# Two FFN products by seven quarter products each, with the second one's activations passed through device memory

## The chip, the cores and the metric

One core of a Trainium2 chip runs the kernel. TensorE (PE) multiplies, VectorE (DVE), ScalarE (ACT) and GpSimd (POOL) do the elementwise work, SyncE (SP) and the other queues issue DMAs. The metric is the device time of one execution: the kernel before took 2033.25 us (median of 3 runs, 2033.06 to 2033.38). All arithmetic is fp32; a product is made from high and low parts of both operands, as three matmuls (high by high, high by low, low by high).

## The reference, cut to what matters

One decoder layer over 1056 rows (a prompt of 1024 and 8 samples of 4), model width 1024. The change touches the last third of it; what goes before (conv, S5 and attention branches, their merge) is left as it is.

```python
x = x + g_m * rmsnorm(merged @ p['w_out'], p['g_post_mix'])
hf = rmsnorm(x, p['g_pre_ffn']) * (1.0 + sc_f) + sh_f
gu = hf @ p['w_ffn_in']                       # 1024 -> 2 * 2816
f = jax.nn.silu(gu[..., :D_FF]) * gu[..., D_FF:]
x = x + g_f * rmsnorm(f @ p['w_ffn_out'], p['g_post_ffn'])   # 2816 -> 1024
```

Outputs are the new x, and states and K/V rows that the earlier stages write.

## The kernel before, in words

Activations lie transposed (features on the 128 partitions, rows along the free axis). A tile of weights is 128 x 128 per matmul; the moving operand is a chunk of 352 rows (three chunks, `csl`), or of 264 rows (four chunks, `lsl`) in the last part.

The program is a list of `Atom`s that `run` (L369) goes through: an atom is one group of matmuls into one PSUM bank. Its evacuation is held back as `pending` and written out after the next atom's matmuls. A `unit` is 512 KB of weights: SP loads it into `raw`, ACT writes the high part `whi` (L396), DVE the low part `wlo` (L397); `ready` allows a unit when a buffer of its ring of three is free. Work beside the matmuls stands in generators that `Side` holds: `advance` steps them by the estimated cost of each atom, and `drain` runs them to their end at that place of the program. Each engine works its own list in the order in which the program wrote it, so what stands first on an engine and waits holds all that is behind it.

- w_out (from `plain(open_r)`): 3 chunks of 8 atoms of 24 matmuls; weights 3 to 7 are kept over the chunks. `sq_gated` squares and gates a bank, `res_gen` (L1826) makes for each finished chunk the two norms, the residual and the modulated input of the FFN, split into `mh` (high) and `ml` (low). Its norms go by way of PE twice: a sum over the partitions (`s<-cst,ss`, `s<-cst,y`), 13 small DVE operations and a diagonal (`rs_dg`), and a matmul that spreads the result (`s<-rs_dg`).
- FFN in and out, in five parts of `PARTS = (4, 4, 5, 4, 5)` tiles of features: for each tile the gate and the up product (24 matmuls of 352 rows for each chunk), tanh, two products on DVE, the split into `fhi` and `flo`; after a part its share of the second product is added into `ya`.
- the last part goes in four chunks of 264 rows, each followed by `last_gen`: norm, residual and output.

In the FFN of the kernel before POOL issues a few DMAs, and shares the last residuals.

Of the kernel before, what the change touches and what calls it, by code (L numbers as in the profile page):

```python
# [16 lines left out]
T = 1056  # L17
# [28 lines left out]
YF = (1.0, 4.0, 0.64)  # L46

# [70 lines left out]
def layout(inp):  # L118
# [3 lines left out]
    o['xT'] = x.reshape(3, CH, 8, 128).transpose(0, 3, 2, 1)  # L122
    c = np.concatenate([g['c_prompt'], g['c_sample']], 0)
# [135 lines left out]
def program(tc, I, O):  # L259
# [39 lines left out]
    xd = dram.tile([128, 8, T], F32, name="xd")  # L299
    numd = [dram.tile([128, 2, TP], F32, name="numd%d" % g) for g in range(2)]  # L300
# [3 lines left out]
    def mm(out, lhsT, rhs, start, stop):  # L304
        return pe.matmul(out=out, lhsT=lhsT, rhs=rhs, start=start, stop=stop)  # L305
# [37 lines left out]

    def kept(box, pool_):

        def get(ask=False):
            if ask:
                return box.get(pool_)
            n_kept[0] += 1
            hi = box[pool_].tile([128, 1024], F32R, name="kh%d" % n_kept[0])  # L350
            if pool_ == 'kp':
                return hi, lo_tile(F32R, "kl")[:, 0:1024]
# [1505 lines left out]
    for c in range(NCH):  # L1858
        for m in range(8):
            u = us[m]  # L1860

            def evac(ps, c, m=m):
# [3 lines left out]
                if m == 7:  # L1866
                    if c:
                        side.drain()
# [162 lines left out]
```

## Time and profile before

| | us |
|---|---|
| median of 3 runs | 2033.25 |
| the profiled execution | 2028.49 |
| its span | 2026.7 |
| from w_out's first matmul to the end (1118.0 to 2026.7) | 908.7 |
| PE busy, share of the span | 96% |
| DVE, ACT, POOL busy | 53%, 29%, 8% |

A stage is read from the views of busy time in stretches; PE counts as busy from a matmul's start to its modelled end, and consecutive matmuls overlap, so the pace of a stage is time divided by count. The idle time in front of an instruction is shown in brackets with what ended it.

### The profile page before, as it was taken

Reading aid. Unit: us, or ns where it says so; the run is one execution under the profiler, and the core shown is the slowest. Engines: PE = TensorE matmul, PEld = TensorE weight load, DVE = VectorE, ACT = ScalarE, POOL = GpSimd, SP = SyncE. Lnnn points to the kernel's source line nnn. Section 1 sums busy time; section 2 is a strip of 40 time slices with the busy share of each in tenths; the row PEclk is TensorE's granted clock in tenths of the full one; section 3 lists DMA queues with packets and bytes.
Section 4 is the critical chain, followed back from the end, with each engine's and each line's share of the span. In section 5 each row is a group of like instructions: output and inputs, shape, how many; then the busy total and the mean of one; then the engine's idle time right before and its main releaser. Section 6 shows DMA issues by size and latency. Waiting matters only on the chain.

```text
span 2026.7 us, 29823 instructions
## 1 busy us (share of the span) xinstructions
PE 1951.0 (96%) x12284; PEld 1824.4 (90%) x12284; DVE 1078.7 (53%) x2256; ACT 586.6 (29%) x1145; POOL 159.6 (8%) x273
## 2 busy tenths in 40 slices
PE   8999999999999899999999998999999999999997
PEld 2899798798876788998999998999999999999996
DVE  5677685474474766654976378312332233232347
ACT  3422422522422542222323344232202111212233
POOL 0000001001000131223200000000000000000023
PEclk9999999999999999999999999999999999999998
DMA  7333134134355544226732222110111011111131
GB/s 286 88 105 108 45 126 147 55 116 154 116 189 195 189 147 138 93 93 188 195 101 80 91 107 79 52 53 32 52 53 42 27 58 53 42 53 41 52 108 76
DMA packets 59847, 203.88 MB, mean 101 GB/s; under 512 B 12372, under 2 KB 13540, under 8 KB 58176
## 3 DMA queue, kind: packets, MB, share of 16 engines
q1 hardware_dynamic: 35264, 110.70, 16.3%
q0 software_dynamic: 17104, 64.82, 9.4%
q10 hardware_dynamic: 7344, 26.47, 3.9%
q8 instruction: 96, 1.57, 0.3%
q14 instruction: 39, 0.32, 0.0%
HBM read 159.87 MB, written 43.00 MB: 100 GB/s over the span
## 4 chain that ended last, share of the span: by engine, by line
PE 56%; DVE 3%; issue 2%; DMA 2%; ACT 1%; POOL 1%; POOLq 0%; DVEq 0%; ACTq 0%
PE z L305 53%; PE s L305 3%; DMA yq<-yd 1%; DVE y L308 1%; POOL Tm L1338 0%; DMA yd<-ysb 0%; DMA raw<-i_wfo 0%; DMA sbw<-i_sb 0%; ACT mh L615 0%; DMA raw<-i_wout 0%; DVE x L1824 0%; DVE wlo L397 0%; DVE ss L308 0%; PE m L305 0%; DVE kl L397 0%
## 5 line engine op out<-in xcount | busy, mean ns | idle before, releaser
L305 PE MATMUL z<-hh,whi 128*128 128x352 f32 x1152 | 380.5, 330 | 2.7 <-ACT hh L615 1.4
L397 DVE SCALAR_TENSOR_TENSOR wlo<-raw,whi 128x1024 fp32r<-128x1024 f32 (+1 forms) x169 | 203.3, 1205 | 329.1 <-ACT whi L396 324.9
L305 PE MATMUL z<-hh,wlo 128*128 128x352 f32 x1152 | 373.1, 324 | 3.1 <-DVE wlo L397 3.1
L305 PE MATMUL z<-hl,whi 128*128 128x352 f32 x1152 | 373.2, 324 | 0.8 <-DVE hl L308 0.8
L305 PE MATMUL z<-mh,whi 128*128 128x352 f32 x1104 | 358.9, 325 | 4.6 <-ACT mh L615 4.6
L305 PE MATMUL z<-ml,whi 128*128 128x352 f32 x1104 | 358.2, 324 | 0.3 <-DVE ml L308 0.2
L305 PE MATMUL z<-mh,wlo 128*128 128x352 f32 x1104 | 357.9, 324 | 0.0
L396 ACT ACTIVATE whi<-raw 128x1024 fp32r<-128x1024 f32 (+1 forms) x169 | 176.0, 1042 | 396.9 <-PE z L305 341.7
L305 PEld LDWEIGHTS z<-hh,whi 128*128 128x128 f32 x1152 | 219.3, 190 | 14.5 <-issue 7.0
L305 PEld LDWEIGHTS z<-hh,wlo 128*128 128x128 f32 x1152 | 219.1, 190 | 3.7 <-DVE wlo L397 3.7
L305 PEld LDWEIGHTS z<-hl,whi 128*128 128x128 f32 x1152 | 219.3, 190 | 2.6 <-DVE hl L308 1.6
L305 PEld LDWEIGHTS z<-mh,whi 128*128 128x128 f32 x1104 | 208.8, 189 | 5.5 <-ACT mh L615 5.1
L305 PEld LDWEIGHTS z<-ml,whi 128*128 128x128 f32 x1104 | 209.0, 189 | 1.7 <-DVE ml L308 1.4
L305 PEld LDWEIGHTS z<-mh,wlo 128*128 128x128 f32 x1104 | 208.8, 189 | 0.0
L305 PE MATMUL z<-fhi,whi 128*128 128x352 f32 (+1 forms) x504 | 161.0, 319 | 2.9 <-DVE ya L308 2.9
L305 PE MATMUL z<-fhi,wlo 128*128 128x352 f32 (+1 forms) x504 | 160.4, 318 | 0.0
L305 PE MATMUL z<-flo,whi 128*128 128x352 f32 (+1 forms) x504 | 160.1, 318 | 0.0
L1498 DVE SCALAR_TENSOR_TENSOR ycv<-cub,vecs,ycv 128x1024 f32<-128x1024 f32 x120 | 153.9, 1283 | 3.1
L305 PEld LDWEIGHTS z<-fhi,whi 128*128 128x128 f32 x504 | 95.4, 189 | 3.2 <-DVE ya L308 3.1
L305 PEld LDWEIGHTS z<-flo,whi 128*128 128x128 f32 x504 | 95.6, 190 | 0.1
L305 PEld LDWEIGHTS z<-fhi,wlo 128*128 128x128 f32 x504 | 95.7, 190 | 0.0
L308 DVE TENSOR_TENSOR tg<-tg,z 128x352 f32<-128x352 f32 x66 | 34.2, 519 | 115.2 <-PE z L305 115.2
(391 smaller groups left out, 2993.4 us busy)
## 6 DMA issues: line engine op xcount, KB each, us to landing
raw<-i_win SPq DMA_DIRECT2D x48, 512.0 KB, 3.6
raw<-i_wfi SPq DMA_DIRECT2D x44, 512.0 KB, 3.4
raw<-i_wmod SPq DMA_DIRECT2D x32, 512.0 KB, 4.3
gd<-g ACTq DMA_DIRECT2D x24, 528.0 KB, 2.9
g<-gd ACTq DMA_DIRECT2D x24, 528.0 KB, 5.0
raw<-i_wfo SPq DMA_DIRECT2D x17, 512.0 KB, 3.5
mw<-i_wmod SPq DMA_DIRECT2D x16, 512.0 KB, 5.9
kc<-i_kc POOLq DMA_DIRECT2D x8, 896.0 KB, 6.2
```

What stands on the lines that cost most here:

```text
L305: return pe.matmul(out=out, lhsT=lhsT, rhs=rhs, start=start, stop=stop)
L308: dve.tensor_tensor(out=out, in0=a, in1=b, op=op)
L396: act.activation(out=hi[:, 0:n], in_=raw[:, 0:n], func=AF.Copy, scale=scale)
L397: dve.scalar_tensor_tensor(out=lo[:, 0:n], in0=raw[:, 0:n], scalar=scale, in1=hi[:, 0:n].bitcast(F32), op0=ALU.mult, op1=ALU.subtract)
L1498: dve.scalar_tensor_tensor(out=a_, in0=ub[:, k:k + TP], scalar=wv[:, k:k + 1], in1=a_, op0=ALU.mult, op1=ALU.add)
```

## The change

Both products of the FFN are cut into 2 x 2 blocks of each operand (1024 = 2 x 512 or 2816 = 2 x 1408 along the sum, the columns in halves, two chunks of 264 rows as a pair; there are two pairs, p = 0 and 1) and made by seven block products with sums and differences of blocks (the variant with 7 products and shared sums).

- w_out and the stage before it go in four chunks of 264 rows. w_out's weights are loaded and split again for each chunk. `res_gen` adds the residual on POOL. After two chunks `x_gen(p)` makes the seven left operands (B11, B21, B22, T1 to T4) of a pair with four POOL subtractions, each split into high and low. Before the last chunk stand an empty atom and `side.drain`.
- FFN in: a job is one tile of gate and the same tile of up, with seven operands of weights, of which four POOL operations make the sums and differences in place (L2003 to L2009). The first 10 of 22 jobs (`EARLY`) run for pair 0, then again for pair 1; the other 12 for both pairs. Product q = 2 is added into the bank of q = 0, q = 5 into that of q = 3, q = 6 into that of q = 4; the DVE collects blocks in one tile `st` for each pair. After a second-half tile POOL makes four differences of the results (L2043) and writes six blocks to device memory `fd`; after a first-half tile it writes one (L2039).
- FFN out: `b_load` reads the blocks from `fd` on POOL's queue, `b_split` splits them; the weight sums are made by POOL (L2156); `out_evac` combines the seven products in `ya`.

```diff
@@ run
         def ready(v, i):
-            keep = units[v][3]
-            if keep:
-                return first[v] <= i + KEEPAHEAD and keep(True) is not None
-            return (len(ring) < 3 or last[ring[-3]] < i) and (v < 2 or first[v - 2] <= i)
+            if any(len(rings[t]) >= 3 and last[rings[t][-3]] >= i for t in tags(v)):
+                return False
+            ahead = 6 if units[v][3] else 2
+            return v < ahead or first[v - ahead] <= i
@@ res_gen
-            residual(y, bc, ks, xc[:, ks])
-            act.activation(out=sq[:, ks], in_=xc[:, ks], func=AF.Square)
+            TT(y[:, ks], y[:, ks], bc[:, 0:LC].unsqueeze(1).to_broadcast([128, 4, LC]), ALU.mult)
+            pool.tensor_tensor(out=xc[:, ks], in0=xc[:, ks], in1=y[:, ks], op=ALU.add)
+            act.activation(out=y[:, ks], in_=xc[:, ks], func=AF.Square)
@@ x_gen
+        def put_parts(name, src):
+            hi, lo = X_[name, p] = place[name]
+            act.activation(out=hi, in_=src, func=AF.Copy)
+            TT(lo, src, hi.bitcast(F32), ALU.subtract)
...
+        put_parts('B11', a11)
+        sub(a11, a12, a11)
+        yield YX
+        put_parts('B21', a21)
+        sub(a12, a22, a12)
+        yield YX
+        put_parts('T1', a11)
+        sub(a11, a22, a11)
+        yield YX
+        put_parts('T2', a11)
+        sub(a21, a21, a11)
...
@@ w_out
+            if m == 7:
+                todo(*[res_gen(c)] + ([x_gen(c // 2)] if c % 2 else []))
...
-    us = [unit(flat(I['wout'][m]), keep=kept(R_, 'wr') if m >= 3 else None) for m in range(8)]
-    for c in range(NCH):
+    for c in range(NLC):
+        if c == 3:
+            plain(lambda: None)
+            plain(side.drain)
         for m in range(8):
...
+            u = unit(flat(I['wout'][m]))
@@ FFN in, one job
+                if q == 0:
+                    job['s'] = R_['fq'].tile([128, 512], F32, tag="s1", name="s1")
+                    pool.tensor_tensor(out=job['s'], in0=u[:, h0], in1=u[:, h1], op=ALU.add)
+                    pool.tensor_tensor(out=u[:, h0], in0=g[:, h0], in1=u[:, h0], op=ALU.subtract)
+                halves(w, (g[:, h0], g[:, h1], g[:, h0], u[:, h0], job['s'], u[:, h1], g[:, h1])[q], 512, 1.0)
+                if q == 0:
+                    pool.tensor_tensor(out=g[:, h0], in0=job['s'], in1=g[:, h0], op=ALU.subtract)
+                if q == 1:
+                    pool.tensor_tensor(out=g[:, h1], in0=g[:, h1], in1=g[:, h0], op=ALU.subtract)
...
+                elif q == 2:
+                    act.activation(out=u2, in_=z, func=AF.Copy)
+                elif q == 3:
+                    TT(u[:, LC:2 * LC], u2, z, ALU.add)
...
+                    TT(g[:, LC:2 * LC], u2, z, ALU.add)
+                    t = ft[:, 2 * b:2 * b + 2].rearrange("p a x -> p (a x)")
+                    act.activation(out=t, in_=g, func=AF.Tanh, scale=0.5)
+                    dve.scalar_tensor_tensor(out=t, in0=t, scalar=1.0, in1=g, op0=ALU.add, op1=ALU.mult)
+                    TT(t, t, u, ALU.mult)
+                    if b == 0:
+                        pool.dma_start(out=fd[0, p, :, a, :], in_=ft[:, 0])
+                    else:
+                        b11, b12, b21, b22, t1, t2, t3, t4 = [ft[:, i] for i in range(8)]
+                        for o, x, y in ((t1, b12, b11), (t3, b22, b12), (t2, b22, t1), (t4, b21, t2)):
+                            pool.tensor_tensor(out=o, in0=x, in1=y, op=ALU.subtract)
+                        pool.dma_start(out=fd[1:7, p, :, a, :].rearrange("q p x -> p q x"), in_=ft[:, 2:8])
...
+                    key = (p, {2: 0, 5: 3, 6: 4}.get(q, q))
+                    first = key[1] == q
+                    if first:
+                        banks[key] = zt()
+                    gemm4(banks[key], w[0], X_[ORDER[q], p], 4, first, True, not first)
...
+    for n in JOBS[:EARLY]:
+        in_job(n, [0])
...
+    for n in JOBS[:EARLY]:
+        in_job(n, [1])
+    for n in JOBS[EARLY:]:
+        in_job(n, [0, 1], last_job if n == JOBS[-1] else None)
@@ FFN out
+        pool.dma_start(out=lo[:, 0:KP[j]].bitcast(F32), in_=fd[OUTORD[o // 2], o % 2, :, k0:k0 + KP[j], :])
...
+                pool.tensor_tensor(out=s, in0=a, in1=b, op=op)
```

On PE, in w_out: of the kernel before, the sums and spreads (`s`) of a finished chunk's norms, each with the row before and behind it.

```order
L305 MATMUL z_10846<-mh_10204,wlo_10043 128x352
L305 MATMUL s_10901<-cst_68,ss_10624 88x1 x4
L305 MATMUL z_10936<-mh_9445,whi_10149 128x352
...
L305 MATMUL z_10972<-mh_10204,wlo_10275 128x352
L305 MATMUL s_11002<-rs_dg_10928,cst_68 128x352
L305 MATMUL z_11007<-mh_9445,kh1_10280 128x352
```

Now, at the drain ahead of the last chunk (ss_11242 and y_11241 are the third chunk's, y_10893 the second's):

```order
L306 MATMUL z_11468<-mh_10364,wlo_11393 128x264
L306 MATMUL s_11497<-rs_dg_11390,cst_68 128x264
L306 MATMUL s_11513<-cst_68,y_10893 88x1 x3
L306 MATMUL s_11541<-rs_dg_11539,cst_68 128x264
L306 MATMUL s_11579<-cst_68,ss_11242 88x1 x3
L306 MATMUL s_11607<-rs_dg_11605,cst_68 128x264
L306 MATMUL s_11619<-cst_68,y_11241 88x1 x3
L306 MATMUL s_11647<-rs_dg_11645,cst_68 128x264
L306 MATMUL z_11665<-mh_9514,whi_11427 128x264
```

Seven `s` steps stand there one behind the other, between the last product of the third chunk and the first of the fourth; before, at least 24 products stood between two of them.

On DVE, in the FFN in. Before, around one tile (`tg`, `flo` of the result, `wlo` of the weights):

```order
L308 TENSOR_TENSOR flo_13762<-tg_13819,fhi_13761 128x352
L397 SCALAR_TENSOR_TENSOR wlo_13851<-raw_13526,whi_13850 128x1024
L1890 SCALAR_TENSOR_TENSOR tg_13881<-tg_13881,z_13822 128x352
L397 SCALAR_TENSOR_TENSOR wlo_13885<-raw_13672,whi_13884 128x1024
L308 TENSOR_TENSOR tg_13881<-tg_13881,z_13856 128x352
```

Now, in a job of the early ones for pair 1 (`wop` are weight operands, raw_13564 and ru_13565 the next job's gate and up weights; z_13701 is the bank of q = 3 and 5, z_13718 that of q = 4 and 6; `st` is where the blocks are collected):

```order
L309 TENSOR_TENSOR wop_13673<-raw_13564,wop_13673 128x512
L309 TENSOR_TENSOR st_13379<-st_13379,z_13659 128x264
L309 TENSOR_TENSOR wop_13693<-raw_13564,wop_13693 128x512
L309 TENSOR_TENSOR wop_13715<-raw_13564,wop_13715 128x512
L309 TENSOR_TENSOR st_13379<-st_13379,z_13701 128x264
L309 TENSOR_TENSOR wop_13732<-ru_13565,wop_13732 128x512
L309 TENSOR_TENSOR st_13379<-st_13379,z_13718 128x264
```

The low part for the next job's q = 2 (wop_13715, from raw_13564) now stands ahead of the evacuation of this job's q = 3 (z_13701).

On POOL, in the FFN in. Before it issues DMAs there, and these rows are all from w_out to the last residuals but for repeats:

```order
L1830 DMA xc<-i_xT 128x2816
L1841 DMA xd<-xc 1024x1x352
L1996 DMA x_16887<-xd 128x4x264
L1823 TENSOR_TENSOR ya<-ya,bs 128x2x264
L1824 TENSOR_TENSOR x_16889<-x_16889,ya 128x528
```

Now, for the same stretch as the rows on DVE (ft_13380 is the tile of results of pair 1; the L2043 rows belong to the job before the one whose banks are z_13701 and z_13718):

```order
L2043 TENSOR_TENSOR ft_13380<-ft_13380 128x264 x4
L2044 DMA fd_76<-ft_13380 128x6x264
L2003 TENSOR_TENSOR s1_13674<-ru_13565 128x512
L2004 TENSOR_TENSOR ru_13565<-raw_13564,ru_13565 128x512
L2007 TENSOR_TENSOR raw_13564<-s1_13674,raw_13564 128x512
L2009 TENSOR_TENSOR raw_13564<-raw_13564 128x512
L2039 DMA fd_76<-ft_13380 128x264
```

The rewriting of raw_13564 (L2007), which the next job's q = 2 is taken from, stands behind the four differences and the DMA of an earlier job's results.

## Rows read from the trace of the kernel before

**Rows 1.** The page, busy time by engine over the span.

```profile
PE 1951.0 (96%) x12284; PEld 1824.4 (90%) x12284; DVE 1078.7 (53%) x2256; ACT 586.6 (29%) x1145; POOL 159.6 (8%) x273
```

**Rows 2.** Busy time in stretches: bounds, length; PE, PEld, DVE, ACT, POOL (counts); clock; DMA share, GB/s.

```profile
1118.00:1231.00 113.00, 109.05 (x673) 106.28 (x672) 68.24 (x143) 46.97 (x87) 3.58 (x5) 0.98 0.29 102
1231.00:1376.00 145.00, 139.47 (x849) 138.12 (x848) 57.12 (x106) 41.80 (x74) 0.86 (x1) 0.98 0.16 54
1376.00:1944.00 568.00, 568.00 (x3517) 568.00 (x3517) 175.14 (x284) 100.92 (x158) 3.52 (x5) 1.00 0.14 46
1944.00:2012.00 68.00, 63.16 (x501) 61.99 (x499) 50.06 (x125) 31.93 (x70) 20.61 (x16) 0.97 0.30 111
```

**Rows 3.** Timeline of PE in the last part: start, duration, matmul, idle before.

```profile
1951.99 0.39 PE L305 MATMUL z<-fhi,whi 128*128 128x264 f32 x1 [2.91 <-DVE ya L308]
...
1953.08 0.42 PE L305 MATMUL z<-flo,whi 128*128 128x264 f32 x1
...
1956.92 0.28 PE L305 MATMUL z<-fhi,sh 128*128 128x264 f32 x1
...
1961.96 0.28 PE L305 MATMUL z<-fhi,sl 128*128 128x264 f32 x1
```

**Rows 4.** The norm chain after the last product: timeline, all engines.

```profile
2012.67 0.60 PE L305 MATMUL s<-cst,ss 128*88 128x1 f32 x6 [1.53 <-DVE ya L308]
2013.31 0.16 DVE L439 TENSOR_SCALAR rs_v<-s 88x3 f32<-88x3 f32 x1 [0.68 <-PE s L305]
...
2016.27 1.22 PE L305 MATMUL s<-rs_dg,cst 88*128 88x264 f32 x2 [3.00 <-DVE rs_dg L463]
2017.52 0.39 ACT L1966 ACTIVATE bs<-s 128x264 f32<-128x264 f32 x1 [4.95 <-PE s L305]
...
2017.99 1.30 POOL L1823 TENSOR_TENSOR ya<-ya,bs 128x528 f32<-128x528 f32 x1 [9.88 <-ACT bs L1966]
```

**Rows 5.** DVE from 1118 us on, by form: count | busy, mean ns.

```profile
L308 DVE TENSOR_TENSOR ya<-ya,z 128x264 f32<-128x264 f32 x32 | 13.1, 422 | 7.0 <-PE z L305 6.7
...
L1823 DVE TENSOR_TENSOR y<-y,s 128x1408 f32<-128x1408 f32 x6 | 9.7, 1614 | 3.6 <-PE s L305 3.6
...
L1823 DVE TENSOR_TENSOR ya<-ya,s 128x528 f32<-128x528 f32 x9 | 6.3, 698 | 2.9 <-ACT bs L1966 2.9
```

**Rows 6.** The tile view of m: duration ns min/median/max.

```profile
L308 DVE TENSOR_TENSOR m<-E,WT x8: 681/684/687, 759.1 to 930.4; 128x512 f32<-128x512 f32 x8
```

**Rows 7.** ACT from 1118 us on, by form.

```profile
L396 ACT ACTIVATE whi<-raw 128x1024 fp32r<-128x1024 f32 x59 | 62.4, 1058 | 198.3 <-PE z L305 160.4 <-issue 37.8
L1894 ACT ACTIVATE fhi<-tg 128x352 fp32r<-128x352 f32 x66 | 32.8, 497 | 205.7 <-DVE tg L308 205.7
...
L1839 ACT ACTIVATE y<-xc 128x1408 f32<-128x1408 f32 x6 | 8.3, 1381 | 31.6 <-DVE xc L1824 31.6
```

**Rows 8.** The page, POOL instructions that issue DMAs: count | busy, mean ns.

```profile
L1338 POOL DMA_DIRECT2D Tm<-Mt x64 | 32.3, 513 | 41.5 <-issue 41.2 <-DMA Tm<-Mt 0.3
...
L1841 POOL DMA_DIRECT2D xd<-xc x3 | 2.6, 861 | 95.5 <-DVE xc L1824 95.5
```

**Rows 9.** Timeline of DVE and POOL (between them other engines) in the last part.

```profile
1971.33 1.21 DVE L1824 TENSOR_TENSOR x<-x,ya 128x528 f32<-128x528 f32 x1
...
1972.05 1.68 POOL L1824 TENSOR_TENSOR x<-x,ya 128x528 f32<-128x528 f32 x1
...
1972.46 0.41 DVE L308 TENSOR_TENSOR ya<-ya,z 128x264 f32<-128x264 f32 x1
...
1972.80 1.22 DVE L308 TENSOR_TENSOR ss<-ss,sq 128x264 f32<-128x264 f32 x1
...
1973.69 1.53 POOL L1823 TENSOR_TENSOR ya<-ya,bs 128x528 f32<-128x528 f32 x1
...
1974.67 1.12 DVE L1824 TENSOR_TENSOR x<-x,ya 128x528 f32<-128x528 f32 x1
```

More of the change, by code (lines that the diff above doesn't have):

```diff
@@ L416, in run @@
                     ns += 1
-                while nd < min(ns + 3, len(units)):
+                while loadable():
                     load(nd)
@@ L1719, in open_m @@
             side.add(gelu)
-    MM = lambda: [M_['m', k] for k in range(8)]
     def tiles(key, n):
@@ L1811, in rest @@
         def rest():
-            if m:
+            if not first:
                 TT(R_['ss', c], R_['ss', c], sq, ALU.add)
@@ L1898, in open_ya, with operand, gemm4 @@
-    def open_ya():
-        side.drain()
-        F_['close_kp']()
+            u = unit(flat(I['wout'][m]))
+            dense(u, range(8), (lambda c=c: [m_parts(k, c) for k in range(8)]), c, wout_evac(m), None,
+                  lambda c: slice(0, LC))
+    F_ = {}
+    ORDER = ('B11', 'B21', 'T2', 'T3', 'T1', 'T4', 'B22')
+    opno = [0]
+    def operand(load, make, ahead):
+        opno[0] += 1
+        return unit(None, op={'load': load, 'make': make, 'ahead': ahead, 'no': opno[0]})
+    def gemm4(ps, w, x, ks, first, last, again=False):
+        for k in range(ks):
+            wh, wl = w[:, k * 128:(k + 1) * 128], w[:, 512 + k * 128:512 + (k + 1) * 128]
+            for i, (a_, b_) in enumerate(((wh, x[0]), (wh, x[1]), (wl, x[0]))):
+                mm(ps[:, 0:LC], a_, b_[:, k], first and k == 0 and i == 0, last and k == ks - 1 and i == 2,
+                   skip_group_check=again)
@@ new lines, in last_gen @@
+    def last_gen(c):
+        yp = F_['yp']
+        xc = F_['x1', c]
+        yield YF[0]
+        dg = rstd_bcast(yp, [R_['ss', c]], 1024, EPS, 3)
+        yield YF[1]
+        bc = rstd_psum(dg, LC)
+        ya = F_['c'][:, :, lsl(c)]
+        last = c == 2
+        bs = yp.tile([128, LC], F32, tag="sq1", name="bs", bufs=2)
+        act.activation(out=bs, in_=bc[:, 0:LC], func=AF.Copy)
+        for i in (3, 0, 2, 1) if not last else (3, 0, 1, 2):
+            ks = slice(2 * i, 2 * i + 2)
+            on_pool = i in (PL if not last else (3,))
+            tt = (pool if on_pool else dve).tensor_tensor
+            r = (bs if on_pool else bc)[:, 0:LC].unsqueeze(1).to_broadcast([128, 2, LC])
+            tt(out=ya[:, ks], in0=ya[:, ks], in1=r, op=ALU.mult)
+            tt(out=xc[:, ks], in0=xc[:, ks], in1=ya[:, ks], op=ALU.add)
+            (act if last and i == 3 else sp).dma_start(out=O['yT'][c][:, ks], in_=xc[:, ks])
+            yield YF[2]
@@ L2006, in program @@
+    b_splits((13, 2))
+    for p in range(2):
+        for mi in range(4):
+            out_atoms(6, mi, (p,))
     plain(lambda: None)
```

539 lines of the change are left out of this document (334 added, 205 removed).

## The prediction

> **What bounds the kernel now.** I read the page's busy times first: PE is busy for 96% of the span, POOL for 8% [rows 1]. Then the view by stretches: from w_out's first matmul at 1118 to 2012 PE is hardly ever idle, and from 1376 to 1944 never: 568 us for 3517 matmuls of 352 rows, 0.1615 us each [rows 2]. So TensorE bounds this part, and fewer columns save time one for one, as long as the others follow. Third I read the timelines for what the new pieces cost: pace of a 264-row matmul, the norm chain, POOL beside DVE. Outside the part from 1118 on the order of each engine is as before, but for the stage just ahead of w_out, which does the same in chunks of 264; I take it at no change (768 matmuls of 264 for 576 of 352 rows).
>
> **What the products save.** 41 steps from 1956.92 to 1961.96 make 0.123 us for a 264-row matmul [rows 3]; I take 0.121, since the 352-row pace would scale to 0.121 (0.1615 x 264 / 352). FFN before: 4392 matmuls of 352 and 480 of 264 rows, 709 + 58 = 767 us. After: 22 jobs x 7 x 2 x 12 = 3696 and 7 x 4 x 2 x 33 = 1848, all of 264 rows: 5544 x 0.121 = 671 us. That is 96 us saved, if nothing waits. w_out stays at 93 us. The rest of this part is about what waits.
>
> **Part 1, w_out's drain.** In the order of PE seven norm steps stand between the third chunk's last product and the fourth's first one, nearly each waiting for DVE (and by it for ACT and POOL). PE can do nothing else there. Durations: a 1056-element DVE operation is three quarters of 1614 ns [rows 5], 1.24 us with its start; ACT's square likewise 1.04 [rows 7]; a POOL add of 528 took 1.30 when nothing held it [rows 4], so 2.6 for 1056. A sum on PE to DVE's first small step is 0.64, from there to the spread 2.96, and the spread 1.25 to its reader [rows 4].
> The end of chunk 1's `res_gen`: spread 1.25, first product 1.24, two POOL adds 5.2, square 1.04, three sums 2.36, sum and small steps 3.6, spread 1.25, two products 2.5, modulation about 1.5: 19.9 us. Then `x_gen(0)`: first two low parts 2.3, four POOL differences 10.4, then one high and two low parts 3.5: 16.2. DVE's list has it ahead of chunk 2's small steps: 2.96, spread 1.25, 1.24, 5.2, 1.04, 2.36, 3.6, 1.25: 18.9. Together 55 us of idle PE. From below 45 (POOL's differences wholly beside DVE's seven low parts, 8.7); from above 58, with the port turns of part 2. I take 55. Six us more go to w_out's other norm steps and a clock drop. Before, PE was busy for 109 of the 113 us of w_out's stretch [rows 2]. W_out now: 93 + 55 + 6 = 154.
>
> **Part 2, FFN in for one pair alone (10 jobs, twice).** A job is 84 matmuls, 10.2 us, 20.3 for a first-half and a second-half tile. POOL, which did next to nothing here (3.52 us in 568, all of it DMA issues) [rows 2], now has a chain that PE needs. The third product's weights of the next job are rewritten by L2007; in POOL's list that stands behind four differences of the preceding job's results and their DMA. On DVE the low part of these weights stands ahead of the evacuation of this job's q = 3, and PE's q = 5 adds into that bank, so must wait for the evacuation. From the end of q = 6 of a second-half job:
> - ACT high part of q = 5 0.63 (512 elements, between 0.50 for 352 and 1.06 for 1024) [rows 7], DVE low part 0.68 [rows 6], evacuation 0.42 [rows 5], tanh 0.62, two operations of 528 at 0.70 [rows 5]; with the gaps 3.9 us;
> - four POOL differences of 264 elements. No row has this size: between 0.65 (half of 1.30) and 1.30; I take 0.72 with the wait between them, since POOL's row grows with the size: 2.9;
> - the DMA's issue between 0.51 and 0.86 [rows 8], here 0.8 for 768 pieces;
> - L2003, L2004, L2007, each waiting for the one before: 1.26 + 0.07, 4.0;
> - ACT 0.63, DVE 0.68, evacuation 0.42: 1.7.
> That is 13.4 us, where q = 5 could start at 5 x 1.45 = 7.3. With q = 5 and 6 (2.9 us) the job takes 16.3. The following job has no differences ahead of L2003, only a DMA (0.5): 3.9 + 0.5 + 4.0 + 1.7 + 2.9 = 13.1 with gaps. The two together 29.4 us instead of 20.3.
> DVE and POOL also stop each other: the POOL add that begins at 1972.05 takes 1.68 instead of 1.30, and DVE's sum of 264 elements from SBUF takes 1.22 instead of 0.42, ending 0.29 after POOL does; the one with a PSUM operand in between takes 0.41 [rows 9]. All low parts are of the first kind. Three turns of some 0.5 us can fall on the chain of a job: 0 to 3.3 us for both, I take 1.5. And after 2.91 us of idle PE the matmuls went from 0.12 to 0.22 us apart for a while (durations 0.42) [rows 3], the 1.2 GHz level: 0.10 us lost on 16 matmuls, 1.6 us, for one or both jobs; I take one. Sum 32.5 for two jobs, ten times: 325 us, and 15 for the last chunk's `res_gen` and `x_gen(1)`, whose two POOL adds and four differences of 2.6 us stand in this chain in the first half: 340. From below 27.5 x 10 + 8 = 283, from above 37 x 10 + 25 = 395.
> The page "GPSIMD Engine Reference" of the Trainium skill speaks against the change: section 4.1 sends elementwise adds to VectorE, about twice as fast for two inputs, and section 3.1 has 4497 ns for 2048 elements. Scaled, my estimate from it would be 1.12 us for 512 and 0.58 for 264 elements: 1.1 us less for two jobs, 11 us less in all.
>
> **Part 3, the other 12 jobs, both pairs.** 168 matmuls, 20.3 us a job. The chain is the same with four more differences and a DMA, but one pair's banks come round after 14 groups instead of 7: its evacuation of q = 3 would come at about 15.4 (no port turns) to 16.7 us where q = 5 of pair 1 starts at 11 x 1.45 = 16.0. So hardly a wait: 12 x 20.3 + 3 = 247 us (244 to 253).
>
> **Part 4, FFN out.** 1848 x 0.121 = 224 us, 32 for each of the seven products. DVE has at most 28 us of work in one (six splits 6.8, twelve low parts 7.7, up to 24 evacuations 10.1 and 8 sums of squares 3.4) and is hidden; POOL's sums of weights (12 x up to 1.26) wait for SP's loads, and the last block of activations of each product is issued behind them, one and a half groups ahead of its use. I add 2 us for each of six changes: 236 (226 to 252). Ends of stages 3 (0 to 5). The tail after the last product is as it was.
>
> **The sum.** 154 + 340 + 247 + 236 + 3 = 980 us in place of 893 (the four stretches are 894 [rows 2], and the last microsecond of them holds no product): 87 more. The span of the profiled execution, 2026.7, becomes 2114, its time (2028.49, 1.8 above the span) 2115; the median of the runs lies 4.8 above that execution, so **2120 us**. The bounds together: 141 + 283 + 244 + 226 = 894 to 160 + 395 + 253 + 252 + 5 = 1065, 2034 to 2205.
>
> **Rivals.**
> - *Faster: POOL keeps up, and only the drain stays.* Weights are prepared five groups ahead on six buffers; if POOL's rewriting were done in that time, two early jobs would take 20.3 us. For it: POOL's work for two jobs is 8 x 1.33 + 4 x 0.72 + 1.3 = 14.8 us, less than 20.3. Against it: its list lets it start late, not the amount. The early jobs take 203 + 20; 154 + 223 + 247 + 236 + 3 = 863, 30 less than now: 2003 us. The point from which it decides: two jobs in under 23.8 us instead of 32.5 ((893 - 154 - 247 - 236 - 3 - 15) / 10).
> - *Slower still: FFN out waits too.* If the loads of blocks land after their split is due, ACT and DVE stand in front of the next weights and PE waits some 8 us at each of six changes instead of 2: 36 more, and with both port turns and both clock drops in part 2 (3.4 for two jobs) 34 more: 2190. For it: a load behind three sums that wait for weights' DMAs; against it: weights are loaded one group of three ahead.
> - *Neither drain nor chain costs:* 863 - 55 = 808, 1948 us. The order of PE speaks against it.
>
> **How the numbers follow.** Forecast 0.62, POOL keeps up 0.16, FFN out waits too 0.19, neither 0.03. What lies within 0.2% cannot be told from no change here. The first case's own range, 2034 to 2205, has next to nothing below 2033, so faster 0.18, same 0.02, slower 0.80. The range goes down to 2000, to take in the first rival, and up to 2195.
>
> **What would show it.** An idle stretch of 45 to 58 us on PE after three quarters of w_out, with POOL's adds and differences in its chain; in the early jobs waits of PE of about 6 and 3 us in turn, ended by DVE's evacuation into `st`, with L2007 on POOL ending the wait of ACT's `wop`; no such waits with both pairs. Early jobs at 20 us for two would make the prediction wrong, and so would products of w_out within the drain.

## The result, and the profile after

The changed kernel takes 2229.08 us (median of 4 runs, 2224.37 to 2230.04), the kernel before 2033.15 in the runs beside it: ratio 1.0964, 95% interval 1.0943 to 1.0985, slower by 196 us. The forecast was 2120, 87 us slower, with 2000 to 2195 as range: slower, as forecast, but by 109 us more, and above the range. The profiled execution has a span of 2226.7 us, 112.7 more than the 2114 forecast for it.

The page after: the line of busy times that answers to [rows 1], then PE's busy tenths in 40 slices of 55.7 us and the clock granted to it.

```profile
PE 1938.1 (87%) x13344; PEld 1798.8 (81%) x13344; DVE 1407.1 (63%) x2691; ACT 767.9 (34%) x1490; POOL 590.8 (27%) x637
...
PE   7999999999998999989996266676669999999976
...
PEclk9999999999899999999998587888889999999987
```

PE, at 96% before, now idles where the tenths fall: once to 2 (w_out's drain), then 6 and 7 over seven slices (the early jobs), 7 and 6 at the end (FFN out's last two products). In the same slices the granted clock falls. The stretches that answer to [rows 2], with bounds found by counting products (768 for w_out, 1680 for the early jobs, 2016 for the late ones, 1848 for FFN out); columns as there:

```profile
0.00:955.80 955.80, 911.97 (x5736) 793.70 (x5736) 596.37 (x1368) 311.06 (x669) 109.64 (x210) 0.97 0.40 131
955.80:1131.00 175.20, 168.49 (x1201) 165.85 (x1201) 129.03 (x242) 55.35 (x102) 18.43 (x35) 0.98 0.47 137
1131.00:1296.70 165.70, 107.37 (x819) 104.55 (x818) 102.51 (x196) 73.25 (x120) 34.65 (x20) 0.80 0.43 138
1296.70:1688.20 391.50, 257.15 (x1698) 248.52 (x1697) 229.79 (x332) 119.72 (x218) 185.54 (x145) 0.83 0.25 82
1688.20:1939.00 250.80, 245.54 (x2019) 244.52 (x2018) 144.23 (x252) 85.59 (x159) 119.31 (x117) 1.00 0.31 104
1939.00:2211.30 272.30, 245.38 (x1873) 240.50 (x1872) 196.66 (x280) 121.11 (x220) 120.30 (x109) 0.92 0.60 200
2211.30:2226.70 15.40, 2.16 (x11) 1.14 (x9) 8.49 (x23) 1.77 (x4) 2.94 (x2) 0.58 0.18 70
```

Of the kernel before, the stretch that answers to the first of these rows, up to the same place in PE's order:

```profile
0.00:946.50 946.50, 904.51 (x5737) 786.73 (x5737) 596.51 (x1368) 311.12 (x669) 109.61 (x210) 0.98 0.39 133
```

Set against the forecast, term by term (us):

| stretch | forecast | measured | difference |
|---|---|---|---|
| start of w_out | 1118 | 1131.0 | +13.0 |
| w_out with its drain | 154 | 165.7 | +11.7 |
| early jobs | 340 | 391.5 | +51.5 |
| late jobs | 247 | 250.8 | +3.8 |
| FFN out, and 3 for ends | 239 | 272.3 | +33.3 |
| behind the last product | 15, as before | 15.4 | about 0 |

**The drain.** PE's timeline from the third chunk's last product on (idle time before a row and its releaser in brackets):

```profile
1211.42 0.61 PE L306 MATMUL s<-rs_dg,cst 88*128 88x264 f32 x2
1225.14 1.01 PE L306 MATMUL s<-cst,y 128*88 128x1 f32 x6 [13.11 <-DVE y L309]
1229.14 1.22 PE L306 MATMUL s<-rs_dg,cst 88*128 88x264 f32 x2 [3.00 <-DVE rs_dg L462]
1230.16 0.95 PE L306 MATMUL s<-cst,ss 128*88 128x1 f32 x6
1255.80 1.22 PE L306 MATMUL s<-rs_dg,cst 88*128 88x264 f32 x2 [24.69 <-DVE rs_dg L462]
1266.93 1.01 PE L306 MATMUL s<-cst,y 128*88 128x1 f32 x6 [9.92 <-DVE y L309]
1270.94 1.22 PE L306 MATMUL s<-rs_dg,cst 88*128 88x264 f32 x2 [3.00 <-DVE rs_dg L462]
1271.58 0.80 PE L306 MATMUL z<-mh,whi 128*128 128x264 f32 x1
```

From 1211.4 to 1271.6 there is not one product, only the seven norm steps in the order foreseen, five of them waiting for DVE (53.7 us in all): 60 us where 55 (45 to 58) were forecast.

**Two early jobs.** DVE, POOL, ACT's high parts and PE in a first-half job for pair 1 (the second-half job before it ends at 1616.7):

```profile
1620.48 1.73 PE L306 MATMUL z<-ml,wop 128*128 128x264 f32 x12 [0.72 <-ACT st L2021]
...
1620.83 3.46 POOL L2043 TENSOR_TENSOR ft<-ft 128x264 f32<-128x264 f32 x3 [8.50 <-DVE ft L309]
...
1624.58 0.86 POOL L2044 DMA_DIRECT2D fd<-ft  x1 [0.30 <-POOL ft L2043]
1625.46 1.27 POOL L2003 TENSOR_TENSOR s<-ru 128x512 f32<-128x512 f32 x1
1626.81 1.26 POOL L2004 TENSOR_TENSOR ru<-raw,ru 128x512 f32<-128x512 f32 x1
1628.15 1.26 POOL L2007 TENSOR_TENSOR raw<-s,raw 128x512 f32<-128x512 f32 x1
1629.44 0.63 ACT L1975 ACTIVATE wop<-raw 128x512 fp32r<-128x512 f32 x1 [6.29 <-POOL raw L2007]
1629.49 1.27 POOL L2009 TENSOR_TENSOR raw<-raw 128x512 f32<-128x512 f32 x1
...
1630.11 1.20 DVE L309 TENSOR_TENSOR wop<-raw,wop 128x512 fp32r<-128x512 f32 x1 [6.44 <-ACT wop L1975]
1631.23 0.42 DVE L309 TENSOR_TENSOR st<-st,z 128x264 f32<-128x264 f32 x1
...
1631.70 3.01 PE L306 MATMUL z<-mh,wop 128*128 128x264 f32 x12 [6.57 <-DVE st L309]
```

This is the chain as it was forecast, link by link: differences, DMA, three sums on POOL, high part, low part, evacuation, then q = 5. It reaches q = 5 at 15.0 us (1616.7 to 1631.7) where 13.4 stood in the working: three differences in a row take 1.15 us each, where four of 0.72 stood (the first of the four needs only the first-half tile's blocks and ran at 1611.15), the DMA takes 1.16 with its wait instead of 0.8, and the low part 1.20 instead of 0.68, while L2009 runs on POOL. What was not foreseen comes behind the wait: the 12 products of q = 5 take 2.8 us, until 1634.50, not 1.45. They run at the 1.2 GHz level. Both products took 5.3 us (2.9 forecast); in the second-half job before, 4.6. Over 15 jobs (the last five of pair 0, the ten of pair 1) two take 36.2 us, not 32.5.

PE's waits (engine, line, releaser: us in total, times, longest) in the early part:

```profile
PE z L306 <- DVE st L309: 109.0, 20, 8.7
...
PE z L306 <- ACT st L2021: 25.4, 20, 5.5
```

**FFN out.** Its seven products take 38.8, 32.0, 32.3, 32.0, 32.5, 49.1 and 55.7 us. Four are as short as their matmuls (32); the first and the last two hold the excess. At the sixth, from the timeline:

```profile
2109.66 0.57 POOL L2085 DMA_DIRECT2D mh<-fd  x1
...
2110.05 3.83 DVE L309 TENSOR_TENSOR ml<-ml 128x1056 fp32r<-128x1056 f32 x1
...
2110.25 2.51 POOL L2156 TENSOR_TENSOR S<-raw,S 128x512 f32<-128x512 f32 x2
...
2114.26 5.29 DVE L309 TENSOR_TENSOR ya<-ya 128x264 f32<-128x264 f32 x2
2114.71 1.08 POOL L2085 DMA_DIRECT2D ml<-fd  x2
2115.80 3.45 POOL L2156 TENSOR_TENSOR S<-raw,S 128x512 f32<-128x512 f32 x3
...
2119.58 0.42 ACT L1813 ACTIVATE sq<-ya 128x264 f32<-128x264 f32 x1 [11.99 <-DVE ya L309]
...
2120.43 1.06 ACT L2089 ACTIVATE ml<-ml 128x1056 fp32r<-128x1056 f32 x1
...
2121.53 1.26 DVE L309 TENSOR_TENSOR ml<-ml 128x1056 fp32r<-128x1056 f32 x1 [1.64 <-ACT ml L2089]
2121.55 0.59 PE L306 MATMUL z<-ml,wop 128*128 128x264 f32 x1 [5.43 <-ACT ml L2089]
```

DVE's split takes 3.83 us, where the next one takes 1.26, and its two sums 5.29, where the shortest of them take 0.43 each, while POOL runs its sums; ACT stands 12 us in front of a square that needs these sums, and the split behind the square is the one PE waits for. At the first product ACT's first evacuation waited 10.3 us for the DMA that writes out the last job's results. ACT's parts of the weights stand behind it, and PE waits for them, then runs 24 products in 5.6 us instead of 2.9. That `ya` lies over the memory of those results is read from the program (their buffers are closed, and the one of `ya` is opened):

```profile
1957.76 0.39 ACT L2180 ACTIVATE ya<-z 128x264 f32<-128x264 f32 x1 [10.32 <-DMA fd<-ft]
...
1959.00 5.81 PE L306 MATMUL z<-ml,wop 128*128 128x264 f32 x24 [3.26 <-ACT wop L1975]
```

### The profile page after: what moved, and what is told of

It is laid out like the page before. It is cut to its first block, busy times and chain, and to the rows that moved or that the text cites. A ratio compares the mean times of both kernels' runs of the same rounds, so it can differ in the third digit from the quotient of the medians.

```text
span 2226.7 us, 33856 instructions
## 1 busy us (share of the span) xinstructions
PE 1938.1 (87%) x13344; PEld 1798.8 (81%) x13344; DVE 1407.1 (63%) x2691; ACT 767.9 (34%) x1490; POOL 590.8 (27%) x637
## 4 chain that ended last, share of the span: by engine, by line
PE 33%; issue 11%; POOL 10%; DVE 9%; ACT 3%; DMA 3%; POOLq 0%; SPq 0%; DVEq 0%; ACTq 0%
PE z L306 30%; POOL ft L2043 3%; PE s L306 3%; POOL raw L2007 2%; POOL s L2003 1%; ACT wop L1975 1%; DVE wop L1979 1%; DVE wop L309 1%; DVE ya L309 1%; DMA raw<-i_wfo 1%; DVE y L309 1%; POOL ru L2004 1%; DVE st L309 1%; POOL raw L2004 1%; POOL xc L1838 1%
## 5 line engine op out<-in xcount | busy, mean ns | idle before, releaser
L306 PE MATMUL z<-ml,wop 128*128 128x264 f32 x2220 | 306.5, 292 | 22.8 <-ACT st L2021 6.7
L306 PE MATMUL z<-mh,wop 128*128 128x264 f32 x1704 | 246.7, 298 | 83.7 <-DVE st L309 57.2
L306 PEld LDWEIGHTS z<-ml,wop 128*128 128x128 f32 x2220 | 289.7, 195 | 27.7 <-ACT st L2021 8.8
L306 PEld LDWEIGHTS z<-mh,wop 128*128 128x128 f32 x1704 | 229.5, 200 | 90.3 <-DVE st L309 60.3
L393 DVE SCALAR_TENSOR_TENSOR wlo<-raw,whi 128x1024 fp32r<-128x1024 f32 x132 | 160.9, 1223 | 164.4 <-ACT whi L392 163.4
L309 DVE TENSOR_TENSOR wop<-raw,wop 128x512 fp32r<-128x512 f32 x160 | 158.3, 999 | 155.3 <-ACT wop L1975 155.0
L1975 ACT ACTIVATE wop<-raw 128x512 fp32r<-128x512 f32 (+1 forms) x220 | 133.0, 617 | 255.1 <-POOL raw L2007 127.0
L392 ACT ACTIVATE whi<-raw 128x1024 fp32r<-128x1024 f32 x132 | 139.2, 1057 | 182.3 <-PE z L306 167.7
L306 PE MATMUL z<-xa,wop 128*128 128x264 f32 x828 | 132.9, 320 | 57.3 <-DVE st L309 57.1
L306 PEld LDWEIGHTS z<-xa,wop 128*128 128x128 f32 x828 | 125.4, 223 | 59.9 <-DVE st L309 59.1
L2043 POOL TENSOR_TENSOR ft<-ft 128x264 f32<-128x264 f32 x88 | 91.3, 1048 | 141.2 <-DVE ft L309 139.4
```

The costliest lines, as they stand in the source:

```text
L309: dve.tensor_tensor(out=out, in0=a, in1=b, op=op)
L392: act.activation(out=hi[:, 0:n], in_=raw[:, 0:n], func=AF.Copy, scale=scale)
L393: dve.scalar_tensor_tensor(out=lo[:, 0:n], in0=raw[:, 0:n], scalar=scale, in1=hi[:, 0:n].bitcast(F32), op0=ALU.mult, op1=ALU.subtract)
L1975: act.activation(out=w[:, 0:n], in_=src, func=AF.Copy, scale=scale)
L2043: pool.tensor_tensor(out=o, in0=x, in1=y, op=ALU.subtract)
```

## The experiments

Each changed kernel ran beside the kernel before (ratio to it with its interval). The lengths of stretches in the table are counted from products in each trace, as above; the kernels that are left out of it differ in FFN out alone; "A" are the ten early jobs of pair 0, "pair" is the mean of two early jobs of pair 1 (mended_early8 has eight of each, and 14 late jobs instead of 12).

| kernel | median us | start of w_out | w_out | A | ten of pair 1 | pair | late | FFN out |
|---|---|---|---|---|---|---|---|---|
| changed | 2229.1 | 1131.0 | 165.6 | 210.5 | 181.0 | 36.2 | 250.8 | 272.4 |
| late_parts | 2135.5 | 1124.9 | 165.6 | 175.7 | 134.2 | 26.8 | 244.9 | 271.7 |
| diffs_behind | 2116.3 | 1127.2 | 167.2 | 164.7 | 124.5 | 24.9 | 246.1 | 269.1 |
| norm_dve | 2122.8 | 1125.6 | 155.1 | 169.3 | 134.3 | 26.9 | 244.9 | 278.0 |
| no_drain | 2204.9 | 1124.7 | 116.0 | 239.1 | 186.0 | 37.2 | 250.9 | 269.3 |
| fill_waits | 2211.2 | 1125.0 | 165.5 | 202.2 | 174.6 | 34.9 | 250.8 | 277.7 |
| norm_spread | 2214.6 | 1126.6 | 165.1 | 200.3 | 180.9 | 36.2 | 250.8 | 273.3 |
| mended | 2103.1 | 1130.6 | 155.8 | 161.2 | 124.6 | 24.9 | 247.9 | 268.4 |
| mended_no_drain | 2092.4 | 1128.7 | 110.9 | 195.8 | 124.5 | 24.9 | 247.3 | 269.9 |
| mended_early8 | 2080.4 | 1125.1 | 111.2 | 170.5 | 98.1 | 24.5 | 288.1 | 268.9 |

Some differences in this table belong to no edit. Ahead of w_out all these kernels have the same program, and w_out starts at 1124.7 to 1131.0. In FFN out, among kernels that change nothing there, the third product takes 32.1 to 32.9 us, but 38.6 in norm_dve and fill_waits; the sixth takes 45.6 to 49.1, the last 53.6 to 55.7.

**late_parts: the order of DVE's list.**

```diff
-            ahead = 6 if units[v][3] else 2
+            ahead = units[v][3].get('split', 6) if units[v][3] else 2
...
-        us = [operand(load if q == 0 else lambda: None, make(q), 6) for q in range(7)]
+        us = [operand(load if q == 0 else lambda: None, make(q), 6, 3) for q in range(7)]
```

> Edit: the high and low parts of an FFN-in operand are made 3 operands ahead of use instead of 6, so that the low part which waits for POOL's rewritten weights no longer stands ahead of the evacuations of q = 3 and q = 4 on DVE. No instruction is added, dropped or moved to another engine. Theory A (the early jobs wait because the order of DVE ties an evacuation to POOL's chain): two early jobs take 22.5 us instead of 36.2 (20.3 of products and about 2 of a wait at q = 2 after a second-half job), the early part 391 becomes about 250, the kernel about 2090 us. Theory B (POOL's amount of work and the port shared with DVE are the bound): the work is the same, two early jobs stay above 30 us, the kernel above 2170 us.

Measured 2135.47 us, ratio 1.0499 (1.0435 to 1.0562); two jobs 26.8 us. The same instructions on the same engines, in another order, take 94 us less, 82 of them in the early jobs (6 are the earlier start of w_out). POOL's list keeps its order but for some steps of the norm; the lists of ACT and DVE change, and the run doesn't part these two. So the wait was tied to the order, as theory A says, though less went than it forecast. What was left stands at q = 2 behind a second-half job; from PE's timeline of this kernel:

```profile
1557.62 4.62 PE L306 MATMUL z<-xb,wop 128*128 128x264 f32 x36 [0.79 <-DVE st L309]
1564.81 2.40 PE L306 MATMUL z<-ml,wop 128*128 128x264 f32 x12 [2.57 <-ACT st L2021]
```

**diffs_behind: the differences' place in POOL's list.**

```diff
-  for o, x, y in (...): pool.tensor_tensor(out=o, in0=x, in1=y, op=ALU.subtract)
-  pool.dma_start(out=fd[1:7, ...], in_=ft[:, 2:8])
+  F_['diffs', p] = diffs        # both are issued at q = 4 of the next job
```

> Edit: as late_parts (operands of FFN in made 3 ahead), and POOL's four differences of a second-half job with their DMA are issued behind the sums of weights of the next job instead of ahead of them. Same work on the same engines. Theory A (what is left of the wait in late_parts is the place of the differences in POOL's list): two early jobs, 26.4 us in late_parts, come to 21 to 23 us, the kernel from 2135 to 2085 to 2105. Theory B (the port that POOL shares with DVE, and POOL's amount): still 25 us or more, the kernel above 2125.

2116.26 us, 1.0402 (1.0363 to 1.0441); two jobs 24.9 us, at B's bound, though the kernel came below B's 2125. The place was worth 2 us for two jobs; PE is left with short waits, here those of the last five jobs of pair 0 and the ten of pair 1:

```profile
PE z L306 <- DVE st L309: 17.1, 28, 1.2
PE z L306 <- ACT st L2021: 6.2, 9, 1.2
```

These are 3.1 us for two jobs. Ahead of the evacuations stand low parts that take up to 1.8 us each (one 2.1) beside POOL's sums, against 0.68 alone.

**fill_waits: the clock.**

```diff
+  if q == 5 and len(prs) == 1:
+      spare = st()
+      for i in range(24):
+          mm(spare[:, 0:LC], w[0][:, 0:128], X_[ORDER[q], p][0][:, 0], i == 0, i == 23)
   gemm4(banks[key], w[0], X_[ORDER[q], p], 4, first, True, not first)
```

> Edit: ahead of q = 5 of each early job PE computes 24 matmuls of 264 rows into a spare bank that nobody reads (2.9 us at full clock), in the time in which it waits for the evacuation of q = 3 anyway; the result isn't touched. Theory A (PE's idle time pulls its clock down, and the half-paced products behind the wait are 4 us of each two jobs): with less idle time the clock stays up, two jobs come from 36.2 to 32 to 34 us, the early part from 391 to 350 to 370. Theory B (the clock falls whatever PE does there, or the 24 matmuls delay q = 5): two jobs stay at 35.5 us or more.

2211.22 us, 1.0872 (1.0815 to 1.0929). PE does 2.9 us more of useless work in each early job, and the early part is 14.7 us shorter. From PE's timeline of this kernel:

```profile
1591.45 3.05 PE L306 MATMUL s<-mh,wop 128*128 128x264 f32 x24
1595.16 1.74 PE L306 MATMUL z<-mh,wop 128*128 128x264 f32 x12 [0.66 <-DVE st L309]
1596.74 4.54 PE L306 MATMUL z<-xb,wop 128*128 128x264 f32 x36
...
1606.49 3.12 PE L306 MATMUL s<-mh,wop 128*128 128x264 f32 x24
1613.30 2.92 PE L306 MATMUL z<-mh,wop 128*128 128x264 f32 x12 [3.68 <-DVE st L309]
```

Where the filling leaves 0.66 us of idle time, q = 5 takes 1.74 us and the job 15.0 instead of 16.5. Where 3.68 are left, q = 5 takes 2.92, and the job goes from 20.3 to 19.6 only. So the half pace comes from PE's own idling and can be held off, and theory A holds in one job of two; its 32 to 34 us for both were too low.

**norm_dve, no_drain, norm_spread: the norm.**

```diff
 norm_dve (on late_parts):
-  pool.tensor_tensor(out=xc[:, ks], in0=xc[:, ks], in1=y[:, ks], op=ALU.add)
+  TT(xc[:, ks], xc[:, ks], y[:, ks], ALU.add)          # and x_gen's differences likewise
 no_drain:
-  if c == 3: plain(side.drain)
+  R_['y', 3] = R_['xb'].tile([128, 8, LC], F32, name="y3")   # x_gen(0) finished ahead of the first job
 norm_spread:
-  yield RY[i] ... yield YX
+  yield RY[i] * (2 if c == 3 else 1) ... yield YX * (1 + p)
```

> Edit: as late_parts, and the norm's residual adds (1056 elements, 2.4 to 2.6 us on POOL) and the differences of pair operands run on DVE. Theory A (POOL's long operations set the drain's length and, in the first five early jobs, stand in the chain ahead of the sums of weights): the drain falls from 60 us to 48 to 53, the first five early jobs from 111 us to 85 to 100, the kernel from 2135 to 2105 to 2115. Theory B (DVE's own list is the bound there, so that the steps only change places): the two change by less than 5 us each.

> Edit: the fourth chunk's w_out results get a buffer of their own, so that the norm steps need not be drained ahead of the fourth chunk; the last operand of pair 1 moves to a freed buffer. Only chunk 1's norm and pair 0's operands are finished ahead of the first FFN job; the other norm steps run beside the early jobs. Theory A: the 60 us of idle PE in w_out goes, 5 to 15 us of it come back ahead of the first job, and 10 to 20 in the early jobs, whose chain on POOL the moved steps lengthen: 2190 to 2210 us. Theory B (the moved steps collide with the early jobs so that nothing is won): 2220 to 2235 us. Theory C (the early jobs have room for them): 2170 us.

> Edit: the steps of the last chunk's norm and of pair 1's operands are issued twice as far apart, over nine of the ten early jobs of pair 0 instead of five. Theory A (each step stands in a chain that is late already, so its time counts wherever it stands): the ten jobs together stay at 205 to 216 us (210.5). Theory B (they cost more because they are bunched): the ten jobs fall to 198 us or less.

norm_dve: 2122.78 us, 1.0434 (1.0389 to 1.0478). The drain falls from 60.3 to 53.3 us, the first five early jobs from 110.9 to 104.5: a part of what A expects, more than B allows; the kernel misses A's 2115, also because FFN out takes 6 us more, which the edit doesn't touch. no_drain: 2204.94 us, 1.084 (1.0774 to 1.0906), within A's range, but not by A's parts: w_out is 49.6 us shorter, and the early jobs are 33.6 longer, about twice what A gave back there. These two make 16 of the 25 us between the profiled executions; 6 are the earlier start of w_out and 3 FFN out, so that the total fits is in part luck. The two stretches of this kernel:

```profile
1124.70:1240.70 116.00, 103.16 (x802) 100.88 (x800) 77.52 (x151) 63.53 (x111) 19.29 (x12) 0.96 0.58 178
1240.70:1665.80 425.10, 270.74 (x1712) 260.35 (x1713) 260.54 (x376) 128.57 (x227) 200.80 (x152) 0.78 0.24 81
```

A step taken out of the drain lands in jobs whose chain is late already. norm_spread: 2214.58 us, 1.0889 (1.0834 to 1.0943); the ten jobs go from 210.5 to 200.3 us, between the two bounds. In the steady jobs ten take 181, so of 29.5 us that the norm costs there about 10 came of bunching, and about 19 stay when it is spread. In late_parts and mended, where the jobs' own waits are short, the ten of pair 0 take 41.5 and 36.6 us more than those of pair 1; so part of the norm's time may have been hidden behind these waits, which no run tests.

**out_sums_dve, out5_sums_dve, out5_left_out: the sixth product.**

```diff
 out_sums_dve:
-  pool.tensor_tensor(out=s, in0=a, in1=b, op=op)
+  TT(s, a, b, op)                         # where the load is issued
 out5_sums_dve: for q == 5 alone, TT(s, a, b, op) right ahead of halves(...)
 out5_left_out: for q == 5 no sum; halves(...) takes the loaded weights
```

> Edit: FFN out's 48 sums and differences of weights (512 or 384 elements) run on DVE instead of POOL. Theory A (the sixth product, q = 5, takes 49 us instead of 32 because a burst of POOL sums holds up DVE's low parts): q = 5 falls to 33 to 36 us, q = 4 rises by up to 4, the kernel is 10 to 15 us faster than 2229. Theory B (loads that land late are the cause): q = 5 stays above 45 us and the kernel within 5 us of 2229.

> Edit: of FFN out's sums only the 12 of the sixth product (q = 5) run on DVE, each just ahead of its operand's high part, where its load has long landed (in out_sums_dve they stood where the load is issued, so DVE waited for DMAs). Theory A (the burst of POOL sums holds up DVE's operations of SBUF alone in q = 5): q = 5 falls from 49 us to 34 to 40, the kernel from 2229 to about 2217. Theory B (DVE has too much work of its own around the change of product, its own sums are no better than POOL's): q = 5 stays at 46 us or more.

> Edit: the 12 sums of the sixth product (q = 5) of FFN out are left out; it takes the loaded weights as they are, so its result is another one. Theory A (POOL's sums, by the port that they share with DVE, hold up DVE and through it ACT's list): q = 5 falls from 49 us to 33 to 37. Theory B (the evacuations of q = 4 and the splits of activations are too much for ACT's and DVE's lists by themselves): q = 5 stays at 43 us or more.

out_sums_dve: 2262.95 us, 1.1125 (1.1059 to 1.1192), slower, which neither theory had: the third product takes 42.3 us and the fifth 66.0. DVE, whose list had no loads to wait for, now stands in front of DMAs; from the waits of this kernel between 2080 and 2150 us:

```profile
DVE raw L309 <- DMA raw<-i_wfo: 30.8, 8, 6.0
```

The sixth takes 44.3, but behind such a fifth this says nothing on its cause. out5_sums_dve: 2227.08 us, 1.0946 (1.0893 to 1.1): the sixth takes 53.0, as theory B has it. out5_left_out: 2218.02 us, 1.0905 (1.0851 to 1.096): 42.1, between the bounds, and 3.5 to 7.0 less than in the kernels that leave FFN out as it is (45.6 to 49.1). So of the 17 us over 32 these few go with POOL's sums; 10 stay without them, behind ACT's and DVE's own lists, as PE's timeline of this kernel has it:

```profile
2116.84 0.59 PE L306 MATMUL z<-mh,wop 128*128 128x264 f32 x1 [4.69 <-ACT mh L2089]
```

**last_norm_dve, pace_last: the last product.**

```diff
 last_norm_dve:
-  on_pool = i in (PL if not last else (3,))
+  on_pool = last and i == 3
 pace_last:
-YF = (1.0, 4.0, 0.64)
+YF = (1.0, 4.0, 1.50)
```

> Edit: the residual steps of the last stage run wholly on DVE for three of four chunks (POOL had half of them). Theory A (POOL's steps hold up DVE's low parts of weights, 1.3 us each instead of 0.6): the last product, q = 6, 55.7 us, falls by 8 to 12 us. Theory B (its weights land late, since the stores stand ahead of the loads in SP's queue): it falls by less than 3 us.

> Edit: in the last stage the four quarters of a chunk's residual are spread over several groups of products (1.5 us of products between two instead of 0.64), nothing else. Theory A (the eight operations in a row on DVE, with POOL's beside them, hold up the low parts of weights): the last product, q = 6, falls from 55.7 us to 44 to 50. Theory B (its weights land late): it stays within 3 us of 55.7.

last_norm_dve: 2223.6 us, 1.0932 (1.0855 to 1.1008); the last product 53.5 us, 2.2 less: by its bound theory B, and no effect of the edit, since kernels that change nothing there have 53.6 to 55.7. pace_last: 2217.08 us, 1.0897 (1.0846 to 1.0948); 48.3 us, 7.4 less, as A has it, and 3 us come back behind the last product (18.4 instead of 15.4). In the last product PE waits 9.0 us for DVE's low parts in the changed kernel, 9.1 in last_norm_dve and 2.1 in pace_last, and 7.3, 6.2 and 1.8 us go at half pace. So the quarters of the residual, issued in a row, hold up the low parts on whichever engine they run. ACT's waits for the loads of these weights come to 4.7, 4.0 and 5.9 us, none over 1.9: late loads can be only a small part of it. PE's waits in the last product of pace_last:

```profile
PE s L306 <- DVE ss L309: 7.0, 1, 7.0
PE z L306 <- DVE wop L1979: 2.1, 2, 1.9
```

The first is a norm sum, `s<-cst,ss`: it stands in PE's own list, and the products behind it start only after it.

**mended, mended_no_drain, mended_early8: together.** The edits of the single runs; of new ones the splits of activations earlier, the place of `ya`, and in the last `EARLY = 8`.

> Edits together: diffs_behind, norm_dve, the last stage's quarters 1.0 us of products apart, FFN out's buffer ya laid above the last job's results (so that its first evacuation needn't wait for their DMA), and FFN out's activations loaded and split one to two groups earlier. The drain stays. By the stages of the single runs: drain 53, w_out 155; early jobs 289 less about 6; late 246; FFN out's first product 38.8 to 33 to 34; its last 55.7 to 48. For the sixth product, q = 5, 49 us, the causes part: if it is the place of the splits in ACT's and DVE's lists behind the results of q = 4, it falls to 33 to 40; if it is the port or DVE's amount, it stays at 46 or more. Sum 2065 to 2085 us.

> Edit: mended, and the buffer of its own for the fourth chunk (no_drain). Theory A (the norm steps that move beside the early jobs cost there about 0.3 to 0.6 of the 50 us won, as in no_drain, where 34 came back): 15 to 35 us less than mended. Theory B (with the lists mended the early jobs take them up nearly free): 40 us or more less than mended.

> Edit: mended_no_drain with 8 instead of 10 jobs for one pair alone. Theory A (a job with both pairs costs its products, one for one pair alone 2 us more): 8 to 12 us less than mended_no_drain. Theory B (the norm steps no longer fit into 8 jobs and are drained ahead of the second pair): no gain, or up to 15 us more.

2103.12 us (1.0351, 1.0276 to 1.0426), 2092.41 (1.0299, 1.0235 to 1.0362) and 2080.43 (1.024, 1.019 to 1.0289). mended missed its range: the first product of FFN out still takes 37.9 us, with the same wait of 10.3 us, so either the place of `ya` is not the cause or the edit left it as it was; this stays open; the sixth takes 44.8, the last 50.0, and the tail 17.4. The third and the fifth take 35.7 and 35.8 instead of 32.3 and 32.5, so on balance the earlier splits win nothing that shows. Without the drain 44.9 us go in w_out and 34.6 come back in A: the kind of cost that theory A has, but 0.77 of the gain instead of 0.3 to 0.6, and the net 11 is below its 15. Two early jobs fewer save 12 us, as expected; in the profiled executions 11 in the jobs, and 4 are the earlier start of w_out. No version here beats the kernel before: what is left of the loss is the norm beside the early jobs, waits at both ends of FFN out, and in mended the drain.

## Why the prediction was right in direction and wrong in size

**Right.** The matmuls: four products of FFN out at 32.0 to 32.5 us (32 forecast) and late jobs of 20.34 us where nothing waits (seven of twelve; the others take 21.7). The drain, with its steps and releasers, 60 us for 55, a little above its bound of 58. The chain of the early jobs, in order and ends: late_parts, which changes nothing but the order, takes 82 us out of it, so what was said against the rival that POOL keeps up holds: it is the order of the lists, not POOL's amount. The sign.

**Wrong, part 1: "six us more" for the rest of w_out.** Outside the drain w_out takes 105.5 us, where 99 stood: PE waits 4.6 us for high and low parts of its weights, one wait of them 3.2, and 37 products at half pace lose 3.6.

**Wrong, part 2: "one clock drop" of 1.6 us for two jobs.** The ten pairs of early jobs take 36.2 us each instead of 32.5: 37 of the 51.5 us, about half of it by this term. Of the 1680 early products 399 start 0.19 to 0.27 us after the one before, the pace of the 1.2 GHz level, and lose 39.6 us against 0.121; ten times 1.6 make 16. In the 15 jobs of the mean it is 3.4 us for two. Nearly each of these waits, of 6.6 and 3.5 us, is followed by such a stretch, also the second, for which the forecast had taken none, though behind these its length varies (1 to 11 of the eleven steps within q = 5). fill_waits shows that it is the wait that does it. The Trainium skill, "TensorE: Matmul & The Clock Gate", section "HAM oscillation — how this bites in real kernels", says as much of waits for DMAs, that each throws PE back to the slow level; this trace agrees. Its rule for the price, half of the slow time, is too high here: from w_out on the clock is at the lower level for 255.3 us, which would be 128, and the products that ran at half pace lose 56, since PE idled in much of the rest.

**Wrong, part 2: the terms of POOL and of the norm.** The differences at 0.72 each (1.15 in a row), and low parts, which in the sum stood at 0.68 and three port turns of 0.5 for two jobs: measured in the two jobs above, q = 5 starts 1.6 and 1.7 us later in its job than forecast without port turns, 3.3 for the 1.5 taken (3.5 in the mean of the 15 jobs). And 15 us for the last chunk's norm were 29.5, of which norm_dve and norm_spread each took some, none all: it counts in DVE's list as well as in POOL's. Two slips of addition carry nothing: the terms of the first chain make 13.3, not 13.4, and the last estimate of part 2 (six sums and four differences at 0.14 us less each) is 1.4 us for two jobs, not 1.1.

**Wrong, part 4: "2 us for each of six changes".** This was the most mis-sized term of all: 12 us, where four changes cost nothing, but the first product takes 6.8 us over its matmuls, the sixth 17.1 and the last 23.7. The rival that let FFN out wait had 36 us in the sum, near the 33 measured, but by another mechanism (late loads at each change), so its nearness is luck. The runs show a wait for the last job's results, POOL's sums beside DVE, the lists of ACT and DVE, and the residual's quarters. 128 products of FFN out ran at half pace, 12.8 us of these, for which the forecast had nothing. Of the last product's 16 us that pace_last leaves, 7.0 are the norm sum in PE's list, 2.1 low parts and 1.8 half pace; the rest is not divided.

**Wrong: "Outside the part from 1118 on [...] at no change".** w_out starts 13 us later. 9.3 of them lie in the first 956 us, with the same instructions (PE's counts differ by one at the bound); PE is busy there for 7.5 us longer (911.97 for 904.51), so its matmuls take longer. Only 1.4 us fall in the stage in chunks of 264 (94.7 for 93.3). The trace has 58.0 us at the lower clock ahead of w_out, in 13 pieces, for 30.7 in 7 before. The experiments, all with the same code there, have 41.0 to 58.0, and w_out mostly starts later with more of it (1124.7 to 1126.6 with 41.0, 1125.6 to 1128.7 with 51.2, 1128.7 and 1130.6 with 58.0). So most of it goes with the clock; what in the change sets off more of these pieces was not tested. It isn't the stage in chunks of 264, since all pieces lie ahead of it.

## What to carry to other kernels

A wait on TensorE can cost twice: its own length, and the products behind it at half pace. Here those of 6.6 us did each time and those of 3.5 in part, while after waits of 0.7 us the twelve products behind took 1.55 us instead of 1.45. Price both, also where the wait falls in work that "only" shifts. Ahead of moving sums to an idle engine, write down which in-order list its result stands in, and what is queued behind that result: here 82 us hung on parts of later weights standing ahead of an evacuation. Steps moved out of an idle stretch are not free if the work beside which they land is late already.

## What was not expected of the hardware

DVE and POOL take turns, but not always one for one. A DVE operation with two inputs, both in SBUF, that begins while POOL is in a sum ended ahead of the end of POOL's next one in 167 of 168 cases of this trace from 1290 us on; one that begins while POOL issues a DMA was passed in 13 of 36 cases by POOL sums behind that DMA, in ten by one (eight of these are low parts, 2.2 us for 0.68), in three by two or three: 3.83 us for a split of 1.26, and 4.46 us, of the 5.29 in the rows above, for the second of two sums of 0.43. The Trainium skill, "SBUF — State Buffer", section "SBUF: two separate sides", has the port go to whichever starts first, for one instruction; that fits the 167, and not these 13.
